# Products queued behind copies on VectorE, and a first row tile loaded in five parts, in a batched trace-of-product kernel

## The chip, the cores and the metric

The kernel runs on one core of a Trainium2 chip. The metric is device time of one execution in microseconds (us), as the median of several runs. A profile of one execution gives the span of the work on the core, which is some 1.8 us shorter than the measured time.

## The reference, cut to what matters

```python
B, N = 8, 2176
a, b = (np.random.randn(B, N, N).astype(np.float32) for _ in range(2))

def reference(a, b):
    prod = np.matmul(a, b)
    traces = np.diagonal(prod, axis1=1, axis2=2).sum(axis=-1)
    return traces.astype(np.float32)
```

The trace of a product is the sum over i and k of `a[i,k] * b[k,i]`. No matrix product is needed: transpose `a`, multiply elementwise with `b`, and sum. Every element is read once, so 303 MB of float32 have to come in.

## The kernel before

`a` comes in row tiles that GpSimd's loads cast to bf16 on the way. TensorE transposes them into PSUM, and ScalarE and VectorE copy two thirds and one third of the results into one large tile `at`. Then `b` comes in, and VectorE multiplies each row block with its part of `at` and sums. For the last batch TensorE takes part of that work.

```python
def load_first(src, start):                      # the very first row tile only
    words = stage.tile([P, DOUBLE * ROWS, N], bf16, tag="stage")
    plain = words.bitcast(f32).rearrange("p r k -> p (r k)")[:, :N]
    half = N // 2
    t = single.tile([P, 1, N], bf16, tag="single")
    nc.sync.dma_start(out=plain, in_=src[start:start + P, :])      # float32, no cast
    nc.scalar.copy(out=t[:, 0, :half], in_=plain[:, :half])
    nc.vector.tensor_copy(out=t[:, 0, half:], in_=plain[:, half:])
    return [(start, 1, t)]
...
def evacuate(dst, src):                          # PSUM -> at, after a transpose
    nonlocal evacs
    if evacs % 3 == 2:
        nc.vector.tensor_copy(out=dst, in_=src)
    else:
        nc.scalar.copy(out=dst, in_=src)
    evacs += 1
...
# per batch: load a, transpose, evacuate ... then, for the rows of b:
    def on_dve(x, y):
        nonlocal cols
        multiply_reduce(x, y, acc[:, cols:cols + 1])
        cols += 1
```

The order of instructions on an engine is not that of the source alone. In the trace the first product of a batch stands ahead of the batch's last copies on VectorE: in batch 1 the product starts at 156.14 us, the last copies at 158.36 and 162.03.

## Time and profile before

| | before |
|---|---|
| median | 711.24 us (711.16 to 711.25, 3 runs) |
| span in the profile | 709.5 us |
| bytes read | 303.04 MB, 427 GB/s over the span |
| busy: PE, VectorE, ScalarE, GpSimd | 29%, 58%, 28%, 5% |
| DMA engines | a digit of 9 (90% or more) in all forty slices but the last |

The last row decides how to read everything else. If the sixteen DMA engines never pause, an earlier copy or product should not shorten the run (the run with the edge alone, below, took 711.11 us against 711.25); only what a DMA engine itself does, or what follows the last landing, should.

The start is this. The view is busy time by stretch; the columns are stretch, length, busy us (and count) of PE, weight loads, VectorE, ScalarE and GpSimd, then granted clock, DMA share and GB/s, counted on the side of the on-chip memory. The first tile's float32 load counts fully there (1.11 MB), the casting loads with half of what they read (150.97 MB; 303.04 MB are read in all).

```profile
3.00:5.00 2.00, 0.00 (x0) 0.00 (x0) 0.00 (x0) 0.00 (x0) 0.65 (x1) 1.00 0.99 418
5.00:9.00 4.00, 1.94 (x9) 1.72 (x9) 0.73 (x1) 1.90 (x2) 0.71 (x1) 1.00 1.07 228
9.00:13.00 4.00, 0.12 (x2) 0.00 (x0) 0.23 (x1) 1.12 (x2) 0.00 (x0) 1.00 1.07 226
13.00:26.00 13.00, 0.00 (x0) 0.00 (x0) 0.00 (x0) 0.00 (x0) 0.00 (x0) 1.00 1.04 222
```

From 3 to 5 us SyncE's load of the first tile runs alone at 418 GB/s; from 5 us on GpSimd's casting loads run at their 222 to 228 GB/s.

### The profile page before, as it was taken

Reading aid. Unit: us, or ns where it says so; the run is one execution under the profiler, and the core shown is the slowest. Engines: PE = TensorE matmul, PEld = TensorE weight load, DVE = VectorE, ACT = ScalarE, POOL = GpSimd, SP = SyncE. Lnnn points to the kernel's source line nnn. Section 1 sums busy time; section 2 is a strip of 40 time slices with the busy share of each in tenths; the row PEclk is TensorE's granted clock in tenths of the full one; section 3 lists DMA queues with packets and bytes.
Section 4 is the critical chain, followed back from the end, with each engine's and each line's share of the span. In section 5 each row is a group of like instructions: output and inputs, shape, how many; then the busy total and the mean of one; then the engine's idle time right before and its main releaser. Section 6 shows DMA issues by size and latency. Waiting matters only on the chain.

```text
span 709.5 us, 3709 instructions
## 1 busy us (share of the span) xinstructions
PE 205.6 (29%) x1406; PEld 192.3 (27%) x1406; DVE 408.9 (58%) x449; ACT 197.3 (28%) x210; POOL 34.7 (5%) x60
## 2 busy tenths in 40 slices
PE   1442006410055100651005600056000660005637
PEld 0432006410055100551005500056000660004636
DVE  0222996129962299523995249942499325993257
ACT  2443005430064200652006610066000660006600
POOL 1000000000010000100001000000000000000000
PEclk9977556775577655776557765577555775557768
DMA  9999999999999999999999999999999999999997
GB/s 220 220 219 217 208 220 220 218 213 211 222 220 217 212 216 218 220 217 214 214 219 220 216 213 216 219 219 216 212 217 220 218 216 212 218 218 215 219 209 140
DMA packets 11620, 152.32 MB, mean 215 GB/s; under 512 B 850, under 2 KB 1106, under 8 KB 3282
## 3 DMA queue, kind: packets, MB, share of 16 engines
q0 software_dynamic: 11456, 150.97, 100.0%
q1 hardware_dynamic: 146, 1.11, 0.5%
q8 instruction: 11, 0.18, 0.1%
q14 instruction: 7, 0.06, 0.0%
HBM read 303.04 MB, written 0.00 MB: 427 GB/s over the span
## 4 chain that ended last, share of the span: by engine, by line
DMA 55%; DVE 34%; issue 7%; another core or an unknown queue 1%; ACT 1%; PE 1%; POOL 0%; DVEq 0%; POOLq 0%
DMA t<-in_b_dram 42%; DVE scratch L121 33%; DMA t<-in_a_dram 12%; DVE at L109 1%; ACT at L111 1%; PE ps L154 0%; DVE acc L121 0%; DVEq L121 0%; POOL identity masks.py:199 0%; PE ps L175 0%; POOL identity masks.py:197 0%; PE total L294 0%; DVE late L121 0%; DVE result L298 0%
## 5 line engine op out<-in xcount | busy, mean ns | idle before, releaser
L121 DVE CUSTOM_DVE_ANT_1 scratch<-at,t 128x2048 bf16<-128x2048 bf16 (+1 forms) x156 | 310.5, 1990 | 112.9 <-DMA t<-in_b_dram 106.4
L111 ACT COPY at<-ps 128x1024 bf16<-128x1024 bf16 x208 | 194.9, 1046 | 485.4 <-PE ps L154 485.4
L154 PE MATMUL ps<-identity,t 128*128 128x128 f32 x1071 | 178.4, 333 | 496.8 <-DMA t<-in_a_dram 291.5
L154 PEld LDWEIGHTS ps<-identity,t 128*128 128x128 f32 x1071 | 164.8, 213 | 506.6 <-issue 283.9
L109 DVE COPY at<-ps 128x1024 bf16<-128x1024 bf16 (+2 forms) x104 | 92.8, 902 | 179.0 <-PE ps L154 171.3
L74 POOL DMA_DIRECT2D t<-in_a_dram x23 | 15.3, 668 | 365.6 <-DVE acc L121 224.6
L74 POOL DMA_DIRECT2D t<-in_b_dram x26 | 16.7, 642 | 288.6 <-PE ps L175 151.9
L175 PE MATMUL ps<-identity,t 128*128 128x128 bf16 x170 | 17.0, 224 | 2.3 <-DVE at L109 1.8
L279 PEld LDWEIGHTS <-at 128*128 128x128 bf16 x153 | 16.9, 117 | 2.2 <-issue 2.1
L279 PE MATMUL trace_ps<-t,at 128*128 128x128 bf16 x144 | 16.2, 288 | 1.4 <-DMA t<-in_b_dram 1.4
L175 PEld LDWEIGHTS <-t 128*128 128x128 bf16 x170 | 13.4, 102 | 4.6 <-issue 4.2
L121 DVE DVE_READ_ACCUMULATOR2_ANT acc<- 128x1 f32 x163 | 13.3, 82 | 0.0
L86 DVE CAST t<-words 128x1088 bf16<-128x1088 f32 x1 | 0.7, 727 | 4.9 <-DMA words<-in_a_dram 4.9
L121 DVE CUSTOM_DVE_ANT_0 scratch<-at,t 128x128 bf16<-128x128 bf16 x7 | 2.0, 291 | 0.2
L85 ACT CAST t<-words 128x1088 bf16<-128x1088 f32 x1 | 1.1, 1098 | 3.8 <-DMA words<-in_a_dram 3.8
L243 POOL DMA_DIRECT2D b_t<-in_b_dram x3 | 1.6, 537 | 7.4 <-PE trace_ps L279 7.4
L121 DVE CUSTOM_DVE_ANT_1 scratch<-at,b_t 128x256 bf16<-128x256 bf16 (+1 forms) x3 | 1.5, 510 | 0.1
L271 DVE TENSOR_REDUCE sums<-acc 128x1 f32<-128x22 f32 (+1 forms) x8 | 1.4, 175 | 0.3
L279 PE MATMUL trace_ps<-b_t,at 128*128 128x128 bf16 x9 | 1.4, 291 | 0.4 <-DMA b_t<-in_b_dram 0.4
L85 ACT ACT_TABLE_LOAD x1 | 1.3, 1283 | 0.7 <-PEq L317 0.7
L294 PE MATMUL total<-late,ones 128*1 128x1 f32 x8 | 0.8, 164 | 0.8 <-DVE late L121 0.8
L294 PEld LDWEIGHTS total<-late,ones 128*1 128x1 f32 x8 | 0.3, 80 | 1.2 <-DVE late L121 1.2
(14 smaller groups left out, 2.7 us busy)
## 6 DMA issues: line engine op xcount, KB each, us to landing
t<-in_a_dram POOLq DMA_DIRECT2D x16, 4352.0 KB, 43.9
t<-in_b_dram POOLq DMA_DIRECT2D x15, 4352.0 KB, 51.7
t<-in_b_dram POOLq DMA_DIRECT2D x9, 544.0 KB, 54.6
t<-in_a_dram POOLq DMA_DIRECT2D x7, 544.0 KB, 44.2
t<-in_b_dram POOLq DMA_DIRECT2D x1, 2176.0 KB, 43.6
words<-in_a_dram SPq DMA_DIRECT2D x1, 1088.0 KB, 5.0
t<-in_b_dram POOLq DMA_DIRECT2D x1, 1088.0 KB, 28.8
b_t<-in_b_dram POOLq DMA_DIRECT2D x1, 256.0 KB, 8.9
```

Source lines behind the costliest of these rows:

```text
L74: issued = nc.gpsimd.dma_start(out=part, in_=rows)
L85: nc.scalar.copy(out=t[:, 0, :half], in_=plain[:, :half])
L86: nc.vector.tensor_copy(out=t[:, 0, half:], in_=plain[:, half:])
L109: nc.vector.tensor_copy(out=dst, in_=src)
L111: nc.scalar.copy(out=dst, in_=src)
L121: nc.vector.tensor_tensor_reduce(out=out, in0=x, in1=y, scale=1.0, scalar=0.0, op0=MUL, op1=ADD, accum_out=acc,)
L154: nc.tensor.transpose(ps[:, n * m + r, :], words[:, r, c0:c0 + step * (P - 1) + 1:step], tiles[f32],)
L175: last_transpose = nc.tensor.transpose(ps16[:, n, r, :], a_t[:, r, c0:c0 + P], tiles[bf16],)
L243: nc.gpsimd.dma_start(out=row[:, lo:hi], in_=b[bi, start:start + P, lo:hi])
L271: nc.vector.reduce_sum(out=tiles["sums"][:, bi:bi + 1], in_=acc[:, :cols], axis=mybir.AxisListType.X)
L279: nc.tensor.matmul(trace_ps, x, y, start=(n == 0), stop=(n == len(pe_work) - 1),)
L294: nc.tensor.matmul(total[:, BATCH - 1:BATCH], tiles["ones"], part, start=(n == 0), stop=(n == len(parts) - 1),)
```

## The change

Two independent intents. First, an ordering edge lets each batch's products queue only behind its last VectorE copy, so that a product waiting for `b` doesn't hold up copies that are ready. Second, the first row tile is loaded by SyncE as 96 partitions and four loads of 8. The source does not say why; the likely aim is to give some DMA engines less work than others.

```diff
+    FIRST_SPLIT = [(0, 96), (96, 104), (104, 112), (112, 120), (120, 128)]
...
-        nc.sync.dma_start(out=plain, in_=src[start:start + P, :])
+        for lo, hi in FIRST_SPLIT:
+            nc.sync.dma_start(out=plain[lo:hi, :], in_=src[start + lo:start + hi, :])
...
     def evacuate(dst, src):
-            nc.vector.tensor_copy(out=dst, in_=src)
+            last_copy = nc.vector.tensor_copy(out=dst, in_=src)
...
+        copies_end = last_copy                  # after the transposes of the batch
...
         def on_dve(x, y):
-            multiply_reduce(x, y, acc[:, cols:cols + 1])
+            with tc.issue_after(copies_end.ins):
+                multiply_reduce(x, y, acc[:, cols:cols + 1])
```

More of the change, by code (lines that the diff above doesn't have):

```diff
@@ L104 @@
     evacs = 0
+    last_copy = None
     def evacuate(dst, src):
-        nonlocal evacs
+        nonlocal evacs, last_copy
         if evacs % 3 == 2:
-            nc.vector.tensor_copy(out=dst, in_=src)
+            last_copy = nc.vector.tensor_copy(out=dst, in_=src)
         else:
```

## The prediction

> **What bounds the kernel now.** I read the page's fortieths row first, then stretches of chosen length, then the chain of waits, then the timeline where the two edited places run.
>
> ```profile
> DMA  9999999999999999999999999999999999999997
> ...
> q0 software_dynamic: 11456, 150.97, 100.0%
> ...
> HBM read 303.04 MB, written 0.00 MB: 427 GB/s over the span
> ...
> L121 DVE CUSTOM_DVE_ANT_1 scratch<-at,t 128x2048 bf16<-128x2048 bf16 (+1 forms) x156 | 310.5, 1990 | 112.9 <-DMA t<-in_b_dram 106.4
> ```
>
> The sixteen DMA engines are busy in every slice but the last. VectorE, the busiest compute engine, is at 58%, and 106.4 of the 112.9 us it idles before products end with a load of `b` landing. Data paces the kernel. The table of issues says how far ahead the queue is:
>
> ```profile
> t<-in_a_dram POOLq DMA_DIRECT2D x16, 4352.0 KB, 43.9
> t<-in_b_dram POOLq DMA_DIRECT2D x15, 4352.0 KB, 51.7
> ```
>
> From the trace's records of loads landing I take that one such load occupies the engines for 20.56 us (successive landings of full loads, all eight batches alike, to 0.05). Landing 44 to 52 us after issue means 23 to 31 us of older work in front of it: a compute delay of a few us cannot starve the queue. So what remains is the start, the end, and how evenly the sixteen engines finish. The end:
>
> ```profile
> 700.00:703.00 3.00, 3.00 (x29) 2.99 (x28) 2.96 (x3) 0.00 (x0) 0.00 (x0) 0.86 1.04 189
> 703.00:704.00 1.00, 1.00 (x12) 1.00 (x10) 0.97 (x3) 0.00 (x0) 0.00 (x0) 0.50 0.56 101
> 704.00:705.00 1.00, 0.80 (x7) 0.56 (x6) 0.96 (x4) 0.00 (x0) 0.00 (x0) 0.50 0.14 24
> ```
>
> (columns: stretch, length, then busy us of PE, weight loads, VectorE, ScalarE, GpSimd, clock, DMA share, GB/s). The share falls 1.04, 0.56, 0.14: the engines do not finish together. A load posts one increment per engine, and their spread in the trace grows from 0.41 us on the first load to 2.47 on the last. The steps of that growth coincide with single packets of 16 and 8 KB on the instruction queues (q8, q14), each of which holds up one engine by some 1.1 or 0.5 us. For the last load the sixteen lags are 0.00, 0.06, 0.20, 0.21, 0.43, 0.57, 0.84, 1.21, then 1.28 to 1.44 for five and 2.19, 2.26, 2.48 for three: eight leaders, eight laggards.
>
> [...] This trace shows no transfer of 8 partitions; the first load of 128 does show 8 packets on each of 16 engines. [...] every instruction packet lies between two loads' packets, at arbitrary places in a load; whether a SyncE load gets in as quickly is not shown, since in this kernel GpSimd's queue starts on each engine exactly when SyncE's share ends (5.06 to 5.46 us). [...] GpSimd's issue of a load has a median of 0.696 us, takes 0.70 inside a product (109.89 us) as well as beside idle VectorE (57.97), and the 20.56 us do not change, so I see nothing to gain there.
>
> **Part one, the order on VectorE.** In batches 1 to 7 the first product stands ahead of the batch's last copies:
>
> ```profile
> 156.14 2.29 DVE L121 CUSTOM_DVE_ANT_1 scratch<-at,t 128x2048 bf16<-128x2048 bf16 x1 [13.05 <-DMA t<-in_b_dram]
> ...
> 158.36 1.55 DVE L109 COPY at<-ps 128x1024 bf16<-128x1024 bf16 x2
> 159.63 0.73 PEld L154 LDWEIGHTS ps<-identity,t 128*128 128x128 f32 x4 [14.22 <-DVE at L109]
> ...
> 162.03 0.22 DVE L109 COPY at<-ps 128x128 bf16<-128x128 bf16 x1
> ...
> 681.97 2.29 DVE L121 CUSTOM_DVE_ANT_1 scratch<-at,t 128x2048 bf16<-128x2048 bf16 x1 [13.14 <-DMA t<-in_b_dram]
> ...
> 687.00 0.53 POOL L74 DMA_DIRECT2D t<-in_b_dram  x1 [15.43 <-PE ps L175]
> ...
> 694.90 1.59 POOL L243 DMA_DIRECT2D b_t<-in_b_dram  x3 [7.37 <-PE trace_ps L279]
> ```
>
> VectorE idles 13.05 us for `b` with copies it could have made, PE waits 14.22 us for a bank, and then 1.55 + 0.22 = 1.77 us of copying breaks into the products. The edge adds no instruction; it moves the 1.77 us into the idle stretch, so each batch's products end some 1.7 us earlier. In batch 7 PE's last transposes come near 672 instead of 686.2, the load issued at 687.00 leaves near 672, and PE's trace matmuls can start when `b` lands, near 682 instead of 686.5. The last three pieces then wait for the four products on the first `b` load: 681.97 + 4 x 2.35 = 691.4, against 694.90. All this is real and hidden: the data engines were full up to 703 and had at least 700 - 696.5 = 3.5 us of backlog when the last piece was issued. VectorE's idle before its last big product at 700.00, now 2.39 us, grows to 2.4 + 1.9 = 4.3 us, because that product still waits for its load. Worth **0.0 us**; I allow 0.2.
>
> **Part two, the first row tile.** One issue of 0.40 us becomes five, 2.0 us on SyncE, which has nothing else to do. Bytes are unchanged. A row of 8704 B takes 0.328 us of one engine (8 rows from 1.8 to 5.1 with a slow first one). [...] +0.66 and -0.66 us for the rest of the run, since nothing ever idles to absorb it. [...] the slowest ends at 2.48 - 0.66 = 1.82 and the slowest leader at 1.21 + 0.66 = 1.87: almost level, and four loads are just the number that does this, which is why I believe that is the aim. The slowest engine sets the landing at about 700.0 that frees the final run of VectorE work: 7.06 us without a pause to 707.06, then PE, one copy and the store to 709.47. That tail is rigid. That landing's eighth and slowest lags are 1.00 and 2.47, so it would come at the later of 1.66 and 1.81 behind the first engine: 2.47 - 1.81 = **0.66 us** off the end. Against it: each small load may cut in between GpSimd's packets, and instruction packets cost some 0.2 us beyond their own time when they do (the packet of 8 KB took 0.32, the next data packet 1.51 instead of 1.30). [...] The copies of the first tile come later, 5.8 to perhaps 4.55 + 4 x (1.30 + 0.33) = 11.1 us, but PE needs the next tile only at 26.66, and the slot that they free is wanted by the data engines only near 46.8.
>
> Sum: 711.24 - 0.66 x my 0.75 belief in the engine numbering and the clean cut, 0.5, gives 710.74, rounded to **710.8 us** because what is cancelled is likelier than more.
>
> **Rivals.** [...] the slowest gets +0.66, time 711.9. Nothing in the trace names an engine; only the fit of the count four speaks for the aim. Second, SyncE's small loads wait behind whole GpSimd loads of 20.56 us, since before, GpSimd's packets stood behind SyncE's whole share. Then the tile is complete only near 47 us, the first slot is freed late, and the queue runs dry for some 3 to 5 us: 715. Instruction packets cutting in at any place speak against it. Third, VectorE becomes free 1.7 us per batch earlier and this adds up, 7 x 1.7 = 12 us, 699: refuted by a busy DMA row and 303.04 MB, which at the steady rate of a 4352 KB load (8.91 MB in 20.56 us, 433 GB/s) need 699 us of transfer plus head and tail.
>
> **Range and chances.** The fitting case gives 710.6, cancelled 711.2, the reverse 711.9; runs scatter by 0.1. Range 710.1 to 712.0. For 2% (14.2 us) either way no mechanism above is large enough; 1% each.
>
> **What would show it.** Right: no product ahead of a copy in a batch, PE's 14 us waits for a VectorE copy gone, VectorE's idle before the last 2048-wide product about 4 us, full-load time still 20.56, last landings' spread below 2.0 us, span down by about 0.5. Wrong: a spread of 3 us or more (numbering reversed), the first tile's cast after 20 us (whole-load arbitration), a DMA digit below 9 near slices 3 or 4, or a batch period shorter than before, which would mean that VectorE's order did set the pace.

Put without engine numbers: eight engines would take two rows more of the first tile than before and the other eight two fewer, which at 0.328 us a row is +0.66 and -0.66 us. If the eight relieved were the laggards, 0.66 us would be won; the rival was that they are not, 711.9 us. One cost is cut as well: four cut-ins of 0.2 us each, 0.8 us, on the eight engines of the small loads, which would cancel the gain. The sum itself stands: 711.24 - 0.66 x 0.75 = 710.74, given as 710.8 us. "Engine numbering" means the assumption that the eight engines of the small loads are not the laggards.

## The result, and the profile after

The changed kernel took **714.12 us** (713.23 to 714.80, 6 runs), the kernel before 711.25 in the same rounds: a ratio of 1.0039, interval 1.0026 to 1.0052. (Ratios here are the mean time of one kernel's runs over that of the other's of the same rounds, so not quite the ratio of the medians.) It is 2.9 us slower, where 0.4 us faster was predicted, and it lies outside the stated range of 710.1 to 712.0.

The profile after is that of the slowest of the six runs (714.80 us, span 713.0 us), so it holds some 0.7 us more than the median. The page after, in the lines that answer to those of before:

```profile
DMA  9999999999999999999999999999999999999996
...
q0 software_dynamic: 11456, 150.97, 99.7%
q1 hardware_dynamic: 178, 1.11, 0.7%
...
HBM read 303.04 MB, written 0.00 MB: 425 GB/s over the span
...
L125 DVE CUSTOM_DVE_ANT_1 scratch<-at,t 128x2048 bf16<-128x2048 bf16 (+1 forms) x156 | 310.6, 1991 | 73.7 <-DMA t<-in_b_dram 66.4
```

The same bytes, engines as full as before, products of the same length. VectorE's wait for `b` fell from 106.4 to 66.4 us. That is the first edit at work: what was idle time in front of a blocked product is now partly in front of copies. The timeline of VectorE in batch 1:

```profile
149.99 0.23 DVE L113 COPY at<-ps 128x128 bf16<-128x128 bf16 x1 [0.89 <-PE ps L179]
159.26 2.29 DVE L125 CUSTOM_DVE_ANT_1 scratch<-at,t 128x2048 bf16<-128x2048 bf16 x1 [9.05 <-DMA t<-in_b_dram]
161.47 0.08 DVE L125 DVE_READ_ACCUMULATOR2_ANT acc<- 128x1 f32 x1
161.59 2.29 DVE L125 CUSTOM_DVE_ANT_1 scratch<-at,t 128x2048 bf16<-128x2048 bf16 x1
```

The last copy now precedes the first product, and products follow each other without a copy between. Yet the first product starts at 159.26 where it started at 156.14: `b` itself arrives 3.1 us later. So the loss is older than batch 1. The stretches of the start:

```profile
3.00:5.00 2.00, 0.00 (x0) 0.00 (x0) 0.00 (x0) 0.00 (x0) 0.65 (x1) 1.00 1.06 270
5.00:9.00 4.00, 0.00 (x0) 0.00 (x0) 0.00 (x0) 0.00 (x0) 0.00 (x0) 1.00 1.23 189
9.00:13.00 4.00, 0.00 (x0) 0.00 (x0) 0.00 (x0) 0.00 (x0) 0.00 (x0) 1.00 0.97 205
13.00:26.00 13.00, 2.06 (x9) 1.71 (x9) 0.95 (x2) 4.31 (x4) 0.72 (x1) 1.00 1.01 216
```

The engines are marked busy (share 1.06), but they move 270 GB/s instead of 418, then 189 instead of 228. So here a busy DMA engine was not always moving data at the rate of before. And the timeline of the first tile:

```profile
0.74 1.78 SPq L87 DMA_DIRECT2D words<-in_a_dram  x5
...
14.73 0.73 DVE L89 CAST t<-words 128x1088 bf16<-128x1088 f32 x1 [13.86 <-DMA words<-in_a_dram]
```

The five issues take 1.78 us in all, and the tile is complete at 14.7 us instead of 5.8. That lateness by itself is hidden; GpSimd's next load leaves at 17.39, long before it is needed.

Reading single packets and landing records out of the trace gives the balance. Each of these loads leaves sixteen landing records, which are read here as one of each engine. In this and later tables, "first big load" is the 4352 KB load of `a` that follows the first tile, "last piece" the last data load of all; for each, the arrival of the first of the sixteen engines, their mean, and the last (us from the span's start):

```
                    first big load           last piece             spread at the end
before              26.02  26.22  26.62      702.69 703.76 705.16   2.48
after               27.03  28.47  30.02      703.57 705.95 708.73   5.16
```

The mean engine is 2.25 us late at 28 us and 2.19 us late at the end, so the whole loss happens in the first tile, and none is won or lost after it. No engine is early. The prediction had expected some engines 0.66 us early.

The packet records show why the rate fell. One row of the first tile is 8704 bytes. Before, from 3.0 us on, nearly every row took 328 ns of its engine. After, the 41 rows that started between 3.5 and 5 us took 515 to 675 ns, and the five that started between 5.5 and 7 us took 1096 to 1222. GpSimd's packets that started before 9 us took 1741 ns in the mean, 2639 at most, instead of 1320.

### The profile page after: what moved, and what is told of

It is laid out like the page before. It is cut to its first block, busy times and chain, and to the rows that moved or that the text cites. A ratio compares the mean times of both kernels' runs of the same rounds, so it can differ in the third digit from the quotient of the medians.

```text
span 713.0 us, 3721 instructions
## 1 busy us (share of the span) xinstructions
PE 206.7 (29%) x1406; PEld 193.2 (27%) x1406; DVE 411.5 (58%) x449; ACT 196.9 (28%) x210; POOL 34.6 (5%) x60
## 4 chain that ended last, share of the span: by engine, by line
DMA 60%; DVE 31%; issue 7%; PE 2%; DVEq 0%; another core or an unknown queue 0%; POOLq 0%
DMA t<-in_b_dram 50%; DVE scratch L125 30%; DMA t<-in_a_dram 11%; PE ps L158 2%; DVE acc L125 0%; DVEq L125 0%; PE ps L179 0%; PE total L301 0%; DVE result L305 0%; DVE late L125 0%; POOLq L76 0%; DVE sums L278 0%; POOLq L324 0%
## 5 line engine op out<-in xcount | busy, mean ns | idle before, releaser
L125 DVE CUSTOM_DVE_ANT_1 scratch<-at,t 128x2048 bf16<-128x2048 bf16 (+1 forms) x156 | 310.6, 1991 | 73.7 <-DMA t<-in_b_dram 66.4
L88 ACT ACT_TABLE_LOAD x1 | 1.3, 1283 | 14.7 <-DMA words<-in_a_dram 14.7
```

The source lines that it names most:

```text
L125: nc.vector.tensor_tensor_reduce(out=out, in0=x, in1=y, scale=1.0, scalar=0.0, op0=MUL, op1=ADD, accum_out=acc,)
```

## The experiments

The theory: **P**, the first tile's split costs DMA time because of the sets of partitions that its loads take: their rows are slower than those of a load of 128. No trace names an engine. Nor can any run here separate the two ends of a transfer: which partitions a load takes also decides which rows of `a` it reads. A load is called crowded below when its rows, past the start-up, take clearly longer than the 328 ns of before. The rivals: **I**, each small load costs a fixed time by cutting in among GpSimd's packets; **O**, the new order on VectorE costs the time.

The kernel before measured 711.22 to 711.25 us. What is read below are differences of 0.6 to 3 us. Where the interval of a ratio reaches down to 1, as for some runs near 712 us, all times of that run still lie above all times of before from the same rounds.

### Each edit alone

The first run has the edge and one load of 128 partitions:

```diff
-        for lo, hi in FIRST_SPLIT:
-            nc.sync.dma_start(out=plain[lo:hi, :], in_=src[start + lo:start + hi, :])
+        nc.sync.dma_start(out=plain, in_=src[start:start + P, :])
```

> The edge that puts products behind copies, with the first tile as one load of 128 partitions. Theory P (the first tile's split loses about 2.2 us of every DMA engine's time before 30 us and the stream never gets it back) and theory I (small loads cut in between GpSimd's packets at a fixed cost each): 711.2 us, as before, last landing near 705.2, spread near 2.5. Rival O (the new order on VectorE costs the time): 714 us.

Measured: 711.11 us (711.08 to 711.72, 5 runs; ratio 1.0000, 0.9988 to 1.0013). The second has the split and the old order:

```diff
-            with tc.issue_after(copies_end.ins):
-                multiply_reduce(x, y, acc[:, cols:cols + 1])
+            multiply_reduce(x, y, acc[:, cols:cols + 1])
```

> The split of the first tile alone, VectorE's order as before. P and I: 713.2 to 714.8 us, first big load landing near 30 us on its slowest engine. O: 711.2 us.

Measured: 714.09 us (713.65 to 714.90, 5 runs; ratio 1.0042). O falls. The order is worth 0.0 us, and the split all of the loss. That the edge did work in the first run is seen on VectorE's timeline:

```profile
146.98 0.23 DVE L112 COPY at<-ps 128x128 bf16<-128x128 bf16 x1 [0.90 <-PE ps L178]
156.64 2.29 DVE L124 CUSTOM_DVE_ANT_1 scratch<-at,t 128x2048 bf16<-128x2048 bf16 x1 [9.43 <-DMA t<-in_b_dram]
```

The last copy is done 9.43 us before `b` comes. In this run the last three pieces were issued at 692.50 instead of 694.90, and the last landing still came at 705.66, against 705.16 (the profiled run is the slowest of its five, 711.72).

### The small loads on every fourth partition, and the tail in one load

Same bytes, same number of loads, but each load of 8 takes every fourth partition:

```diff
-    FIRST_SPLIT = [(0, 96), (96, 104), (104, 112), (112, 120), (120, 128)]
+    FIRST_SPLIT = [(0, 96, 1), (96, 128, 4), (97, 128, 4), (98, 128, 4), (99, 128, 4)]  # lo, hi, step
```

> Both edits, but the four loads of 8 take every fourth of the partitions 96 to 127 instead of 8 neighbours; same bytes, same number of loads[...]. [...] the small loads no longer crowd, 712 to 713 us. P in the form 'the load of 96 is what is slow' and I: unchanged, about 714 us.

Measured: 712.37 us (712.08 to 712.40, 4 runs; ratio 1.0015). Merely choosing other partitions took back 1.75 us of the change's 2.87. All 32 rows of the small loads took 341 ns, and GpSimd's early packets 1318 ns in the mean. They still cut in: the last of these rows starts at 15.7 us. So I, a fixed cost per small load, falls as the main cause. But the edit changed the order of packets as well. The issue of a small load took 0.62 to 0.76 us instead of 0.27 to 0.35, and each of its rows came behind a packet of GpSimd's, while in the changed kernel sixteen of the 32 came directly behind rows of SyncE's. How much of the 1.75 us belongs to the partitions and how much to this order was not separated. The load of 96 was still slow: its rows from 3.4 us on took mostly 500 to 580 ns.

Then the last 32 partitions in one load:

```diff
+    FIRST_SPLIT = [(0, 96, 1), (96, 128, 1)]
```

> Both edits, but the last 32 partitions in one load[...]. If the shape of the load of 96 is the cost: its rows still take about 580 ns instead of 328, 6 x 0.25 = 1.5 us are lost, 712.5 to 713 us. If the loads of 8 are the cost (I): about 711.5 us.

Measured: 712.78 us (712.36 to 713.14, 4 runs; ratio 1.0022). There is no load of 8 here, yet 1.7 us are lost against the run with the edge alone. The rows of the 96 took 490 to 610 ns once the engines were in step, and the sixteen rows that started last, all of them of the 32, took 581 to 919. Why the rows of the 96 take as long as 500 to 600 ns was not shown.

### The same number of partitions, another set

The sharpest pair keeps the count and changes the set. Both runs begin with a load of 64 partitions. In the first they are partitions 0 to 63, in the second 32 to 95.

```diff
+    FIRST_SPLIT = [(0, 64, 1), (64, 128, 1)]                # first run
+    FIRST_SPLIT = [(32, 96, 1), (0, 32, 1), (96, 128, 1)]   # second run
```

> Both edits, but the first tile as partitions 0 to 63, then 64 to 127[...]. Theory P [...] every row takes about 0.65 us instead of 0.33, the tile takes 2.6 us longer, 713.5 to 714 us. Rival S (the loads of 8, or uneven engines, are the cost): 711.2 to 711.6 us, rows 0.33 us.

> Both edits, but the first tile as partitions 32 to 95, then 0 to 31, then 96 to 127[...]. P: the first 64 rows at 0.33 us, the other 64 at up to 0.65 us, 1.3 us longer than one load, 712.3 us. [...]

Measured: 711.92 us (711.72 to 712.40) and 711.88 us (711.72 to 712.02), 4 runs each. As times these are a miss: 713.5 to 714 and 712.3 had been expected. The row times were as expected. Rows of the first load in order of start, sixteen at a time, median in ns:

```
                              rows 1-16  17-32  33-48  49-64
partitions 0 to 63 first          714     328    617    693
partitions 32 to 95 first         890     328    328    338
```

(The first sixteen hold the start-up in all kernels; before, they were at 911. The next sixteen begin while other engines are still in their first row.) Once in step, the rows of partitions 0 to 63 took 617 and 693 ns, about twice the 328 and 338 of partitions 32 to 95. Both loads read 64 rows that lie next to each other in `a`, so being neighbours cannot be the reason here.

What I had wrong is what comes before and after these first loads. First, the issue of a first load of 64 took 0.54 and 0.61 us, against 0.38 with one load of 128, and the first row started at 2.07 and 2.14 us instead of 1.75: of the 0.8 us that both runs lose against the edge alone, 0.3 to 0.4 are this later start, which no theory here had foreseen. Second, in the run with two halves the second load cost next to nothing. In its packet records one row of the second load and one packet of GpSimd's alternate as soon as GpSimd's packets are there. These rows took 341 ns, although up to 14 of them were in flight at once, and GpSimd's packets before 9 us stayed at 1301 ns. So a second load of 64 neighbours was not slow where its rows alternated with other packets; the first load, with row directly after row, was. Third, in the other run the crowding came one load later: 20 of the 32 rows that started next, by their order those of partitions 0 to 31, took 400 to 772 ns. So the two runs come out alike: each has one slow load, the first run its first and the second run its second. The stretch from 3 to 5 us, first of the run with partitions 0 to 63 first, then of the run with 32 to 95:

```profile
3.00:5.00 2.00, 0.00 (x0) 0.00 (x0) 0.00 (x0) 0.00 (x0) 0.65 (x1) 1.00 1.35 292
```

```profile
3.00:5.00 2.00, 0.00 (x0) 0.00 (x0) 0.00 (x0) 0.00 (x0) 0.65 (x1) 1.00 1.08 357
```

Both stretches hold the first of GpSimd's packets already, which count half, so 418 cannot be reached; the row times above are the cleaner reading.

### Small loads by themselves, and which engines they burden

Here the tile comes as one load of 128 again, and four extra loads of 8 partitions go into a spare place that nothing reads. They differ only in which partitions they take: neighbours, every fourth, or every sixteenth.

```diff
+        nc.sync.dma_start(out=plain, in_=src[start:start + P, :])
+        spare = words.bitcast(f32).rearrange("p r k -> p (r k)")[:, N:2 * N]
+        for lo, hi, by in EXTRA:
+            nc.sync.dma_start(out=spare[lo:hi:by, :], in_=src[start + lo:start + hi:by, :])
# (96,104,1), (104,112,1) ...  |  (96,128,4), (97,128,4) ...  |  (0,128,16), (1,128,16) ...
```

> Both edits but the tile in one load of 128, and then four extra loads of 8 neighbouring partitions into a spare place that nothing reads. P: [...] 713 to 714 us. I (fixed cost per small load): the same as the run with spread partitions.

> The same with the four extra loads each taking every fourth partition[...]. [...] the end hardly moves: 711.3 us, last spread about 2.4 us; [...] up to 712.5 us, spread near 3.8 us. I: as the run with neighbours.

> One load of 128 and four extra loads of 8 partitions 16 apart[...]. Theory P: [...] about 712.6 us, rows of the first burst between 0.34 and 0.7 us. Theory 'neighbouring partitions are what is slow': as every fourth, 712.3 us with rows of 0.34.

Measured: 713.25 us (713.07 to 713.65), 712.29 (712.18 to 712.49) and 712.33 (712.19 to 712.53), 4 runs each. Of the neighbours' 32 rows seven took 718 to 1168 ns, and the rest 328 to 513; of the spread ones all took 341. Neighbours cost 0.96 us more for the same bytes. The seven are not of the first small load, whose eight rows took 328 ns each, but of the second, where it came directly behind the first. In the run with every fourth partition a packet of GpSimd's came before each row of the small loads, and with every sixteenth before all but those of the first. So these runs, too, differ in the order of packets as well as in the partitions.

The third run is a miss for P in the form of the expectation, which wanted it between the other two, and is just what was written down beforehand for its rival 'neighbouring partitions are what is slow': 712.3 us. Its rows took 326 to 341 ns, although the eight of the first small load started close together, between 5.05 and 5.38 us. For the small loads it therefore stays open whether neighbourhood (in the on-chip memory or in `a`), something else about the set or the order of packets makes them slow. The pair of the loads of 64 doesn't depend on it.

The run with every fourth partition also answers the prediction's question which engines are the laggards. In its expectation 711.3 us was for the case that the engines of the small loads are not the laggards, up to 712.5 for the case that they are. Four rows of 341 ns are 1.36 us for each engine that takes a row of every small load. The sixteen lags behind the first engine, in us:

```
first big load   0.00 0.10 0.13 0.14 0.15 0.23 0.28 0.46 | 1.49 1.53 1.58 1.59 1.60 1.62 1.68 1.68
load at 286 us   0.00 0.08 0.13 0.18 0.24 0.34 0.45 1.30 | 1.49 1.54 1.56 1.65 1.80 2.64 2.70 2.75
last piece       0.00 0.45 1.16 1.20 1.22 1.31 1.35 1.37 1.41 1.52 1.62 1.83 2.08 3.67 3.74 3.79
```

At the start they stand in two groups of eight, 1.03 us or more apart, so the later eight are those of the small loads. Followed from load to load, each step takes one engine out of its place, by some 1.1 us at most, when one packet of an instruction queue passes. By 286 us one of the early group has moved to 1.30, its other seven still stand below 0.46, and the eight of the later group have spread to between 1.49 and 2.75. From there to the end the three at 2.64 to 2.75 stay the three slowest, with all others at 2.15 or less. Before, the three slowest ended near 2.2 to 2.5; 2.3 and 1.4 make the 3.7. So the three engines that finish last are among the eight that the small loads use. If the change's small loads go to the same eight, which no trace names, it gave more rows to the very engines that were already last.

### The uneven share without the crowding

```diff
+    FIRST_SPLIT = [(32, 96, 1), (0, 32, 4), (1, 32, 4), (2, 32, 4), (3, 32, 4), (96, 128, 1)]
```

> Both edits, with the uneven share of the change [...] but little crowding: partitions 32 to 95 in one load, 0 to 31 as four loads of every fourth partition, 96 to 127 in one load. In the run with extra spread loads the three slowest engines of the end all belonged to the eight that the loads of 8 use. If that is so here, the uneven share alone costs 2 x 0.33 = 0.66 us plus some crowding in the last load: 711.9 to 712.3 us. If the prediction's aim (relief of the laggards) worked once crowding is gone: 710.6 us.

Measured: 711.98 us (711.93 to 712.06, 5 runs; ratio 1.0011, 0.9997 to 1.0024). The first big load shows eight engines within 0.22 us and eight at 1.35 to 1.56, which fits ten rows of the first tile against six, four rows of 0.33 us, as intended. The rows took 328 to 380 ns but for the first sixteen. The last piece ends with a spread of 4.03 us instead of 2.48, the three slowest at 3.39, 3.46 and 4.03. So even with little crowding this split loses 711.98 - 711.11 = 0.87 us. Not all of that is the uneven share: here, too, a load of 64 comes first, its first row starts at 2.16 us instead of 1.75, and the mean engine is late by 0.36 us (26.11 to 26.47). The early eight arrive at 25.81 in the mean and the late eight at 27.13, which is 0.66 us to either side: the prediction's shift of two rows, to the digit. By this reading some 0.4 us are the later start and some 0.5 the uneven share. The arrivals of the runs that carry the sum:

```
                         first big load           last piece             spread at the end
edge alone               25.90  26.11  26.84      702.53 703.64 705.66   3.13
uneven, little crowding  25.69  26.47  27.25      702.40 704.07 706.44   4.03
96, small loads spread   25.79  26.78  27.90      702.36 704.34 706.47   4.11
split alone              26.68  28.34  29.80      703.56 705.82 707.54   3.97
```

Each step down the first three rows moves the mean of the first big load later, and the last row moves it by far the most. By measured times, from the edge alone to the changed kernel: 0.87 us to the uneven split with little crowding (711.11 to 711.98), 0.39 more with the load of 96 (to 712.37), 1.75 more with small loads on neighbouring partitions (to 714.12), together 3.01. Since the load of 96 starts as early as one of 128, at 1.77 us, the later start of some 0.4 us is in the first term and not in the second: read as causes, they are nearer to 0.5 for the uneven share and 0.8 for the load of 96. This is an estimate, and the order in which one takes the terms apart is mine: beside an uncrowded load of 128, small loads of neighbours cost 0.96 more than spread ones, so the terms influence each other.

No version here beats the kernel before: the edge alone ties with it.

## Why the prediction was wrong

**What bounds the kernel: right.** The DMA stream sets the time, and a delay of its first microseconds is never made up: 2.25 us of mean lateness at 28 us is 2.19 at 705.

**Part one, 0.0 us: right.** The edge alone measured 711.11 against 711.25. Its steps were near: copies ahead of products; PE's longest wait for a VectorE copy down from 14.8 to 0.5 us; the last pieces issued at 692.50 for an expected 691.4; VectorE's idle before the product at 700 grew to 3.11 us rather than 4.3, because another 0.79 of idle fell to an earlier product that waits for its own load.

**Part two, the cost of a row: the step that failed first.** "A row of 8704 B takes 0.328 us of one engine" was measured in a load of 128 partitions and carried over to loads of 96 and 8. There rows took 0.5 to 0.7 us and up to 1.2. Instead of +0.66 and -0.66 us, every engine was late, by 1.0 us for the first and 3.4 for the last to arrive. The term of slower rows, absent from my sum, was some 2.1 to 2.5 us (0.39 or 0.8, and 1.75). That rows of these loads are slower is shown. That the set of partitions, with the rows of `a` that go with it, can do it is shown by one pair of loads of 64 (617 to 693 ns against 328 to 338); for the loads of 96 and 8 the reason stays open.

**The engine numbering: wrong too.** I gave 0.75 to two things together, the laggards being outside the eight engines of the small loads and a clean cut, because the count four made a neat balance. In the run with every fourth partition the three slowest, 3.67 to 3.79 us behind the first, are inside. A number that fits an aim is no evidence that the aim is met. The sum also left out what the other 0.25 would cost: with the rival's +0.66 us there it gives 710.9, not 710.74. That rival said 711.9; with little crowding it measured 711.98, in part by luck, since some 0.4 us of that are the later start. And the sign that I named for it, a spread of 3 us or more at the end, doesn't tell: the profile of the edge alone has 3.13.

**Waiting among GpSimd's packets: right in kind.** SyncE's rows cut in between single packets and didn't wait for whole loads: sixteen of them started between 7.7 and 12.4 us, while GpSimd's first load ran until 30.02. The first tile's cast came at 14.7 us for an expected 11.1, and as expected this was hidden.

**The range failed** because its slow side held one thing only, the reversed numbering. Nothing in it stood for a load of another shape running at another rate.

## What to carry to other kernels

Here the DMA engines never paused, and the edit to compute order was worth nothing (711.11 us against 711.25), while time that the DMA engines lost was added at the end, even time lost at the very start (2.25 us at 28 us, 2.19 at the end). When a load is cut or reshaped along partitions, do not carry the old time per row over (328 ns became 515 to 675 here, and up to 1222): compare packet durations and the order of packets, since the busy share did not show the crowding (1.06 at 270 GB/s, 0.99 at 418). Look also at when the first packet starts: the loads of 64 cost 0.3 to 0.4 us there, which could pass for something else. Before giving some engines more work, find out by a harmless extra load which engines are last.
